# The rows of a small triangular inverse over more slots, and one preparation step a slot later

## The chip, the cores and the metric

The kernel runs on one core of a Trainium2 chip. The metric is the device time of one execution in microseconds (us), as the median over timed runs: 3366.95 us for the kernel before (three runs, 3363.61 to 3374.13). The profiled execution is a run of its own.

## The reference

One layer of a diffusion backbone works on 256 context tokens and 256 latent tokens, each with 2048 channels. It has a feed-forward block (`swiglu_a`), a token mixer, and a second feed-forward block (`swiglu_b`, latent tokens only), each with a modulation in front and a layer norm behind. The change lies in the mixer. There 16 heads of 64 channels run a delta-rule recurrence, over the context tokens first and then over the latent tokens, in both directions (d = 0 forward, d = 1 reverse):

```python
def step(s, inp):
    r_t, v_t, w_t, k_t, a_t, b_t = inp
    sa = jnp.einsum('bhvk,bhk->bhv', s, a_t)
    s = (s * w_t[:, :, None, :] + sa[..., None] * b_t[:, :, None, :]
         + v_t[..., None] * k_t[:, :, None, :])
    return s, jnp.einsum('bhvk,bhk->bhv', s, r_t)
...
for d in range(2):
    s_c, y_c = wkv_scan(r_c, v_c, *dirs_c[d], s_zero, reverse=(d == 1))
    _, y_x = wkv_scan(r_x, v_x, *dirs_x[d], s_c, reverse=(d == 1))
```

Beside the recurrence a gated MLP works on the other 1024 channels, and one projection `w_out` joins both.

## The kernel before, in words

All weights are read as fp32 in 512 KB pieces (`wsplit`): SP loads `raw`, ScalarE (ACT) casts the high part `whi`, VectorE (DVE) makes the low part `wlo`, in the mixer in turn with GpSimd (POOL). Three matmuls (`mm3`, L311 to L313) make one product. There are three buffers of `raw` and four each of `whi` and `wlo`.

In the mixer the recurrence is turned into matrices over chunks of 64 tokens. A *unit* u is one pair of heads t = u // 2 in one direction d = u % 2; there are 16. Each unit passes through three generators:

- `begin(u)` runs `prologue` (d = 0 alone, three slots) and `prep`. `prep` makes decays by a scan (`zp`, `pf`, L732 to L733), exponentials, `kd`, `nb` (L743 to L745), `bk`, `ar`, `wn` (L754 to L770), the products `px` with their masked results `aa` and `ra` (L796 to L806), writes parts of `aa` to DRAM (`scr`, L825) and reads them back, spread over all partitions, as `abc` (L837, 1 MB, one buffer).
- `inverse(u)` inverts the unit-triangular matrices. `small_inverse` does the 16 by 16 blocks row by row on DVE: for each of 15 rows one multiply with `abc` (L851) and one reduce (L852), each needing the row before. Then `Rt` (L865) and four rounds of small matmuls (`pX`, `pR`, L875 to L914) double the size twice and give `R`.
- `finish(u)` runs `solve`: `pu` with `R` (L939), the transition matrices `gi` and `wc` from `pg` (L963 to L976), `pq`, then seven state steps `pS` and `S` (L1004 to L1011) with outputs `y`; for d = 1 also a group norm and the epilogue.

The loop over u runs three of them side by side, `finish(u)`, `begin(u + 2)` and `inverse(u + 1)`, so an even unit holds a d = 0 `finish` and `begin` and a d = 1 `inverse`, an odd unit the opposite. `together` calls each generator once in turn, up to its next `yield`; one such pass is a *slot*, counted from 0. After each slot `burst()` issues some steps of independent matmuls (projections of later heads, the gated MLP, `w_out`) from a queue, so many that the queue should last to the end. At the start of an even unit the projections that its `begin` needs are drained from the queue first. Ahead of the loop a *lead-in* runs `begin(1)` with `inverse(0)`.

The order that each engine sees is set by a planner that starts from the order of the program and its own times; each engine then runs its instructions in that order. `behind()` keeps DVE instructions of `prep` and of the rows after the last instruction marked `urgent` (S, gi, wc, y, aa and a few others). Before the change `inverse` yields twice and then the rows go four to a slot, three in the last:

```python
            if n % 4 == 3:
                yield
```

Of the kernel before, what the change touches and what calls it, by code (L numbers as in the profile page):

```python
# [43 lines left out]
def fl(ap):  # L44
    names = " ".join(f"a{i}" for i in range(len(ap.shape) - 1))
    return ap.rearrange(f"p {names} -> p ({names})")
# [7 lines left out]
def tile_layer(ctx: ExitStack, tc: tile.TileContext, x, c, ctx_in, c_ctx, w_ada, b_ada, ln_g, ln_b,  # L54
# [16 lines left out]
    def ps_v(name):  # L71
        return psum.tile([P, 512], F32, tag="v", name=name, bufs=3)
# [7 lines left out]
    def pre(name, shape=(P, 512), dt=F32):  # L80
        return sp.tile(list(shape), dt, tag="pre", name=name, bufs=PRES)
# [7 lines left out]
    def own(name, shape=(P, 512), dt=F32, bufs=1):  # L89
        return sp.tile(list(shape), dt, tag=name, name=name, bufs=bufs)  # L90
# [610 lines left out]
    def behind():  # L701

        return tc.issue_after(urgent[0].ins) if urgent[0] is not None else nullcontext()
# [11 lines left out]
    def prep(t, d, k, r, kk, vt, ups, kdx, s):  # L715
# [15 lines left out]
        with behind():  # L731
            nc.vector.tensor_reduce(zp[:, :, 0], zp[:, :, 1:L // 2 + 1], axis=AX.X, op=ALU.add, negate=True)  # L732
            nc.vector.tensor_tensor_scan(fl(pf), fl(m65), fl(zp), 0.0, op0=ALU.mult, op1=ALU.add)  # L733
        yield
        sgn = -KAPPA if d == 0 else KAPPA
        e = pre("e", (P, NCH, L + 1))
        nc.scalar.activation(fl(e), fl(pf), AF.Exp, scale=sgn)
# [103 lines left out]
    def small_inverse(d, s):  # L841

        x = own("x16", (P, 8, 16), bufs=2)
        sub = own("a16", (P, 8, 16))
        for z in (x, sub):
            nc.scalar.copy(z, i16.unsqueeze(1).to_broadcast([P, 8, 16]))
        for n, i in enumerate(range(14, -1, -1) if d == 0 else range(1, 16)):
            lo, hi = (i + 1, 16) if d == 0 else (0, i)
            r = slice(i, 16) if d == 0 else slice(0, i + 1)
            with behind():  # L850
                nc.vector.tensor_tensor(sub[:, :, lo:hi], x[:, :, lo:hi], s["abc"][:, i, :, lo:hi], op=ALU.mult)  # L851
                nc.vector.tensor_reduce(x[:, :, i], sub[:, :, r], axis=AX.X, op=ALU.add)  # L852
            if n % 4 == 3:
                yield
        s["x16"] = x

    def inverse(d, s):

        aa = s["aa"]
        for _ in range(2):  # L860
            yield
        yield from small_inverse(d, s)

        Rt = own("Rt", (P, 8, 32))
        nc.vector.tensor_tensor(Rt.rearrange("p j (b t) -> p j b t", t=16), s["x16"].unsqueeze(2).to_broadcast([P, 8, 2, 16]),  # L865
                                mh[:, 0, :].unsqueeze(1).unsqueeze(3).to_broadcast([P, 8, 2, 16]), op=ALU.mult)
        R1 = own("R1", (P, 8, 32))
        nc.vector.transpose(R1, Rt)
        yield
        yield  # L870
        pX = ps_v("pX")
        for i in range(8):
            for b in range(4):
                sb = slice(32 * b, 32 * b + 32)
                nc.tensor.matmul(pX[sb, 32 * i:32 * i + 32], aa[sb, b // 2, i // 4, i % 4, 32 * (b % 2):32 * (b % 2) + 32],  # L875
                                 Rt[sb, i, :], start=True, stop=True)
        Z = own("Z", (P, 8, 32))
        urgent[0] = nc.vector.tensor_tensor(Z, pX[:, 0:256].rearrange("p (i t) -> p i t", t=32),
                                ml[d].unsqueeze(1).to_broadcast([P, 8, 32]), op=ALU.mult)
        yield  # L880
        pR = ps_v("pR")
        for i in range(8):
            for b in range(4):
                sb = slice(32 * b, 32 * b + 32)
                nc.tensor.matmul(pR[sb, 32 * i:32 * i + 32], Z[sb, i, :], R1[sb, i, :], start=True, stop=True)
        nc.vector.tensor_tensor(fl(R1), pR[:, 0:256], fl(R1), op=ALU.add)

        Rt = own("Rt", (P, 8, 32))
        nc.vector.transpose(Rt, R1)
        R = own("R", (P, 8, L))  # L890
        nc.vector.tensor_tensor(R.rearrange("p j (b t) -> p j b t", t=32), R1.unsqueeze(2).to_broadcast([P, 8, 2, 32]),
                                mh[:, 1, :].unsqueeze(1).unsqueeze(3).to_broadcast([P, 8, 2, 32]), op=ALU.mult)
        fa, fb = (0, 32) if d == 0 else (32, 0)
        yield
        pX = ps_v("pX2")
        for i in range(8):
            for q in range(2):
                sa, sb = slice(64 * q + fa, 64 * q + fa + 32), slice(64 * q + fb, 64 * q + fb + 32)
                nc.tensor.matmul(pX[sb, 32 * i:32 * i + 32], aa[sa, q, i // 4, i % 4, fb:fb + 32], Rt[sa, i, :],
                                 start=True, stop=True)  # L900
        Z = own("Z", (P, 8, 32))
        for q in range(2):
            sb = slice(64 * q + fb, 64 * q + fb + 32)
            pz = pX[sb, 0:256].rearrange("p (i t) -> p i t", t=32)
            if q:
                nc.scalar.copy(Z[sb], pz)
            else:
                nc.vector.tensor_copy(Z[sb], pz)
        yield
        pR = ps_v("pR2")  # L910
        for i in range(8):
            for q in range(2):
                sa, sb = slice(64 * q + fa, 64 * q + fa + 32), slice(64 * q + fb, 64 * q + fb + 32)
                nc.tensor.matmul(pR[sa, 32 * i:32 * i + 32], Z[sb, i, :], R1[sb, i, :], start=True, stop=True)  # L914
        for q in range(2):
            sa = slice(64 * q + fa, 64 * q + fa + 32)
            pz = pR[sa, 0:256].rearrange("p (i t) -> p i t", t=32)
            if q:
                nc.scalar.copy(R[sa, :, fb:fb + 32], pz)
            else:  # L920
                nc.vector.tensor_copy(R[sa, :, fb:fb + 32], pz)
        s["R"] = R
# [179 lines left out]
    def begin(u):  # L1102
        t, d = u // 2, u % 2
        if d == 0:
            shared[t] = {}
            yield from prologue(t, shared[t])
        sh = shared[t]
        unit[u] = {}
        yield from prep(t, d, xs[t, 0], xs[t, 2], sh["kk"], sh["vt"], ups[t], sh["kdx"], unit[u])
        yield  # L1110
# [185 lines left out]
    put(gate_low())  # L1296
    gens[1, 2] = put(project(1, 2))
    together(begin(1), inverse(0, unit[0]))
    begun(1)
    gm = []  # L1300
# [3 lines left out]
    for u in range(nu):  # L1304
        t, d = u // 2, u % 2
        pace[0] = left[0] / (nu - u + REST) / SLOTS
        if t + 2 < NRT:
            for i in ((0, 2) if d == 0 else (1,)):
                gens[t + 2, i] = put(project(t + 2, i))
            put(gm.pop(0))  # L1310
        if u == 12:
            drain()
            put(tail())
        chains = [finish(u)]
        if u + 2 < nu:
            if d == 0:
                for i in range(3):
                    drain(gens[t + 1, i])
            chains.append(begin(u + 2))
        if u + 1 < nu:  # L1320
            chains.append(inverse((u + 1) % 2, unit[u + 1]))
        together(*chains)
        if u + 2 < nu:
            begun(u + 2)
# [219 lines left out]
```

## Time and profile before

| | us |
|---|---|
| timed runs, median | 3366.95 |
| profiled execution | 3355.58 |
| its span, first to last instruction | 3353.9 |
| PE busy in the span | 3180.8 |
| mixer's lead-in, from 1745.0 | 50.6 |
| mixer's loop over units, from 1795.6 | 789.4 |

Times in the trace count from the span's start. PE is TensorE, PEld its weight loads, SP the engine that issues nearly all DMAs. "Busy" of PE is the union of its matmuls' spans. The granted clock is the share of full speed that TensorE was given; 1.00 is the 2.4 GHz level and 0.50 the 1.2 GHz level. A line of busy time by stretch has, in this order: the stretch, its length, the busy us of PE, PEld, DVE, ACT and POOL (with the number of instructions), the granted clock, the DMA engines' share, and GB/s. A wait names the instruction that waited and, behind the arrow, the one that ended the wait.

### The profile page before, as it was taken

What the parts mean: (1) busy time and instruction counts of PE and PEld (TensorE: products, weight loads), DVE (VectorE), ACT (ScalarE), POOL (GpSimd) and SP (SyncE); (2) the same over time, 40 slices, a digit from 0 to 9 for tenths busy, and PEclk for the clock granted to TensorE, in tenths of its full rate; (3) what the DMA queues carried; (4) which work ended last, traced back from release to release, by engine and by line L of the source; (5) the groups of instructions that cost most, each with busy time, mean ns of one, the idle gap of its engine ahead of it and who ended that gap; (6) DMA issues with size and microseconds to landing.
All of it is one profiled execution on the core that took longest, in us unless ns stands there. A gap on an engine that the chain in (4) does not pass through costs nothing. (4 is left out here: it accounts for less than half of the span.)

```text
span 3353.9 us, 55585 instructions
## 1 busy us (share of the span) xinstructions
PE 3180.8 (95%) x21224; PEld 2537.6 (76%) x21224; DVE 2111.1 (63%) x4253; ACT 1265.4 (38%) x2225; POOL 437.1 (13%) x393
## 2 busy tenths in 40 slices
PE   8999999999999999999888988898898999999997
PEld 3556877787878878788787777777787888888886
DVE  2345676967557565533867667666776756656568
ACT  2321222222222222222464444544443554444443
POOL 2100000000000000000463333333323000000003
PEclk9999999999999999999988999998898999999999
DMA  8866465757647566433354353434553766666664
GB/s 289 271 201 203 146 177 158 215 168 232 195 145 234 155 192 195 129 94 100 114 158 124 98 120 97 111 97 110 127 128 105 227 209 194 188 189 189 190 188 148
DMA packets 562515, 554.36 MB, mean 165 GB/s; under 512 B 42383, under 2 KB 415284, under 8 KB 560200
## 3 DMA queue, kind: packets, MB, share of 16 engines
q1 hardware_dynamic: 561800, 550.61, 55.0%
q8 instruction: 167, 2.74, 0.3%
q14 instruction: 100, 0.82, 0.1%
q0 software_dynamic: 384, 0.17, 0.0%
q10 hardware_dynamic: 64, 0.02, 0.0%
HBM read 543.35 MB, written 7.35 MB: 164 GB/s over the span
## 5 line engine op out<-in xcount | busy, mean ns | idle before, releaser
L299 ACT CAST whi<-raw 128x512 fp32r<-128x512 f32 (+1 forms) x1366 | 839.4, 618 | 1707.6 <-PE po L312 352.4
L302 DVE TENSOR_TENSOR wlo<-raw,whi 128x512 fp32r<-128x512 f32 (+1 forms) x1188 | 826.2, 698 | 687.8 <-ACT whi L299 678.1
L302 POOL TENSOR_TENSOR wlo<-raw,whi 128x512 fp32r<-128x512 f32 x178 | 240.9, 1356 | 2491.0 <-ACT whi L299 2464.7
L311 PE MATMUL po<-ahi,whi 128*128 128x512 f32 (+1 forms) x768 | 292.6, 381 | 3.8 <-DVE X L417 3.1
L313 PE MATMUL po<-ahi,wlo 128*128 128x512 f32 (+1 forms) x768 | 291.1, 379 | 3.6 <-DVE wlo L302 3.6
L312 PE MATMUL po<-alo,whi 128*128 128x512 f32 (+1 forms) x768 | 292.3, 381 | 0.0
L311 PE MATMUL pgate<-h,whi 128*128 128x512 f32 x704 | 277.9, 395 | 2.0 <-ACT h L307 1.6
L311 PE MATMUL pup<-h,whi 128*128 128x512 f32 x704 | 278.0, 395 | 0.9 <-ACT whi L299 0.9
L313 PE MATMUL pup<-h,wlo 128*128 128x512 f32 x704 | 275.3, 391 | 1.0 <-DVE wlo L302 0.9
L313 PE MATMUL pgate<-h,wlo 128*128 128x512 f32 x704 | 275.1, 391 | 0.2 <-DVE wlo L302 0.2
L312 PE MATMUL pgate<-h,whi 128*128 128x512 f32 x704 | 274.7, 390 | 0.0
L312 PE MATMUL pup<-h,whi 128*128 128x512 f32 x704 | 274.5, 390 | 0.0
L417 DVE SCALAR_TENSOR_TENSOR X<-po,modc,X 128x256 f32<-128x256 f32 x352 | 155.1, 479 | 155.4 <-PE po L313 150.4
L274 DVE SCALAR_TENSOR_TENSOR vt<-xk,wa,vt 128x512 f32<-128x512 f32 x256 | 187.3, 748 | 30.2 <-DMA xk<-in_w_ada_dram 28.5
L311 PEld LDWEIGHTS po<-ahi,whi 128*128 128x128 f32 x768 | 145.9, 190 | 43.3 <-issue 7.7
L274 DVE SCALAR_TENSOR_TENSOR vt<-xv,wa,vt 128x512 f32<-128x512 f32 x224 | 163.7, 748 | 23.2 <-DMA xv<-in_w_ada_dram 21.7
L311 PEld LDWEIGHTS pgate<-h,whi 128*128 128x128 f32 x704 | 132.1, 188 | 53.7 <-ACT whi L299 12.2
L312 PEld LDWEIGHTS po<-alo,whi 128*128 128x128 f32 x768 | 146.0, 190 | 35.2 <-issue 7.5
L311 PEld LDWEIGHTS pup<-h,whi 128*128 128x128 f32 x704 | 132.2, 188 | 51.7 <-ACT whi L299 14.9
L313 PEld LDWEIGHTS po<-ahi,wlo 128*128 128x128 f32 x768 | 146.1, 190 | 33.0 <-DVE wlo L302 4.2
L311 PE MATMUL pp<-h,whi 128*128 128x256 f32 (+1 forms) x448 | 158.6, 354 | 4.1 <-ACT whi L299 2.9
L313 PE MATMUL pp<-h,wlo 128*128 128x256 f32 (+1 forms) x448 | 152.9, 341 | 5.2 <-POOL wlo L302 2.6
(389 smaller groups left out, 6264.0 us busy)
## 6 DMA issues: line engine op xcount, KB each, us to landing
raw<-in_ffn_b_wi_dram SPq DMA_DIRECT2D x176, 512.0 KB
raw<-in_ffn_a_wi_dram SPq DMA_DIRECT2D x156, 512.0 KB
xv<-in_w_ada_dram SPq DMA_DIRECT2D x256, 256.0 KB
xk<-in_w_ada_dram SPq DMA_DIRECT2D x256, 256.0 KB
raw<-in_w_in_dram SPq DMA_DIRECT2D x110, 512.0 KB
raw<-in_ffn_a_wo_dram SPq DMA_DIRECT2D x96, 512.0 KB
raw<-in_ffn_b_wo_dram SPq DMA_DIRECT2D x88, 512.0 KB
abc<-scr SPq DMA_DIRECT2D x16, 1024.0 KB
```

Source lines behind the costliest of these rows:

```text
L274: nc.vector.scalar_tensor_tensor(acc[v], raw, csil[:, kt, v:v + 1], acc[v], op0=ALU.mult, op1=ALU.add)
L299: nc.scalar.copy(hi, r)
L302: (nc.gpsimd if turn[1] and turn[0] % turn[1] == 0 else nc.vector).tensor_tensor(lo, r, hi.bitcast(F32), op=ALU.subtract)
L311: nc.tensor.matmul(o, wh, ah, start=start, stop=False)
L312: nc.tensor.matmul(o, wh, al, start=False, stop=False)
L313: nc.tensor.matmul(o, wl, ah, start=False, stop=stop)
L417: nc.vector.scalar_tensor_tensor(xs, po[:, sl], gc[:, d:d + 1], xs, op0=ALU.mult, op1=ALU.add)
```

## The change

The 15 rows are spread differently, and `prep` yields once more for d = 1, after the scan.

```diff
@@ prep @@
         yield
+        if d == 1:
+            yield
         sgn = -KAPPA if d == 0 else KAPPA
...
@@ small_inverse @@
-            if n % 4 == 3:
+            if n + 1 in ((3, 6, 9, 12) if d == 0 else (3, 5, 8, 11, 13)):
                 yield
...
@@ inverse @@
-        for _ in range(2):
-            yield
+        if d == 0:
+            for _ in range(3):
+                yield
         yield from small_inverse(d, s)
```

By slot:

| | before | after, d = 0 | after, d = 1 |
|---|---|---|---|
| rows in slot 0, 1, 2, ... | 0, 0, 4, 4, 4, 3 | 0, 0, 0, 3, 3, 3, 3, 3 | 3, 2, 3, 3, 2, 2 |
| `Rt` in slot | 5 | 7 | 5 |
| `pX`, `pR`, `pX2`, `pR2` in slots | 7 to 10 | 9 to 12 | 7 to 10 |
| `prep`, d = 1: scan; `kd`; `bk`, `ar`; `aa` in slots | 0; 1; 2; 4 and 5 | | 0; 2; 3; 5 and 6 |
| `prep`, d = 1: `scr`; `abc` in slots | 6; 7 | | 7; 8 |
| `prep`, d = 0: scan; `kd`; `bk`, `ar`; `aa` in slots | 3; 4; 5; 7 and 8 | as before | |

## Rows read from the trace of the kernel before

**Rows 1.** The page: busy time of the engines; granted clock in 40 slices.
```profile
PE 3180.8 (95%) x21224; PEld 2537.6 (76%) x21224; DVE 2111.1 (63%) x4253; ACT 1265.4 (38%) x2225; POOL 437.1 (13%) x393
PEclk9999999999999999999988999998898999999999
```

**Rows 2.** Busy time by stretch (columns above): lead-in, mixer's loop.
```profile
1745.00:1795.60 50.60, 41.00 (x515) 34.40 (x511) 36.20 (x85) 20.54 (x38) 16.00 (x14) 0.90 0.51 116
1795.60:2585.00 789.40, 701.58 (x9643) 589.44 (x9642) 543.93 (x1576) 366.08 (x694) 259.91 (x227) 0.94 0.44 112
```

**Rows 3.** PE's waits in the mixer's loop: us in total, times, longest.
```profile
PE pS L1004 <- DVE S L1011: 13.3, 11, 2.3
...
PE px L796 <- DVE ar L764: 9.1, 4, 3.1
...
PE pX L875 <- DVE Rt L865: 6.5, 7, 2.2
...
PE px L796 <- DVE a L851: 4.3, 2, 3.2
...
PE px L796 <- DVE x L852: 2.1, 3, 1.4
...
PE pS L1004 <- DVE x L852: 1.3, 1, 1.3
PE pu L939 <- issue: 0.8, 1, 0.8
```

**Rows 4.** PE's waits in the lead-in.
```profile
PE px L796 <- DVE aa L806: 7.4, 2, 5.8
```

**Rows 5.** DVE in order of time in unit 2: start, us, instruction.
```profile
1926.38 1.16 DVE L851 TENSOR_TENSOR a<-x,abc 128x80 f32<-128x80 f32 x1
...
1927.73 0.48 DVE L743 TENSOR_SCALAR kd<-ic,hcol 128x512 f32<-128x512 f32 x1
...
1930.66 0.73 DVE L851 TENSOR_TENSOR a<-x,abc 128x96 f32<-128x96 f32 x1
1931.31 0.90 DVE L764 TENSOR_TENSOR ar<-xr,e 128x256 f32<-128x256 f32 x1
```

**Rows 6.** PE in order of time, same place; in brackets the idle time before.
```profile
1932.36 0.68 PE L796 MATMUL px<-ar,bk 64*128 64x128 f32 x6 [2.79 <-DVE ar L764]
```

**Rows 7.** Busy time and granted clock around that wait (columns as above).
```profile
1926.00:1933.00 7.00, 4.21 (x39) 3.13 (x37) 6.93 (x19) 3.63 (x7) 3.72 (x4) 1.00 0.25 77
1933.00:1939.80 6.80, 6.80 (x109) 5.33 (x108) 4.02 (x15) 0.59 (x2) 1.99 (x2) 0.50 0.06 19
```

**Rows 8.** DVE's groups, 1795.6 to 2530: busy us, mean ns, idle before.
```profile
L851 DVE TENSOR_TENSOR a<-x,abc 128x8 f32<-128x8 f32 (+14 forms) x225 | 83.2, 370 | 2.3
...
L852 DVE TENSOR_REDUCE x<-a 128x8 f32<-128x16 f32 (+14 forms) x225 | 49.7, 221 | 2.6
```

**Rows 9.** DVE in order of time: the last reduce of unit 3's inverse.
```profile
1987.01 0.28 DVE L852 TENSOR_REDUCE x<-a 128x8 f32<-128x128 f32 x1
```

**Rows 10.** SP in order of time, units 1 and 3: issues of DMAs.
```profile
1886.00 0.63 SPq L837 DMA_DIRECT2D abc<-scr  x1
...
1981.08 5.09 SPq L825 DMA_DIRECT2D scr<-aa  x8
...
1987.66 0.80 SPq L837 DMA_DIRECT2D abc<-scr  x1
1988.51 9.26 SPq L294 DMA_DIRECT2D raw<-in_w_in_dram  x2
```

**Rows 11.** Busy time by stretch behind that load of unit 1 (columns as above).
```profile
1889.00:1898.00 9.00, 6.52 (x111) 4.50 (x101) 3.58 (x16) 0.98 (x2) 0.70 (x1) 0.81 0.53 126
1898.00:1900.00 2.00, 1.26 (x7) 0.73 (x5) 1.63 (x2) 0.36 (x1) 1.57 (x2) 1.00 0.00 0
```

**Rows 12.** DVE in order of time at the start of unit 4 (from 2000.3).
```profile
2006.45 0.69 DVE L302 TENSOR_TENSOR wlo<-raw,whi 128x512 fp32r<-128x512 f32 x1 [5.02 <-ACT whi L299]
2009.89 1.00 DVE L659 SCALAR_TENSOR_TENSOR xk<-pp,mus,xk 128x255 f32<-128x255 f32 x2 [2.75 <-ACT xk L656]
```

## The prediction

> **What bounds the kernel now.** I read the page first, then the table by stage, then who waits for whom on PE, then the order of instructions around single waits. On the page PE is busy 95% of the span and the digit of its granted clock falls to 8 in five slices alone, all of them between 21 and 31 (1677 to 2599 us) [rows 1]. The stage table says why: in the mixer's main loop, 789.4 us long, PE is busy 701.6 us, so 87.8 us are idle, and the mean clock is 0.94, which takes another (1 - 0.94) x 789.4 = 47 us of full speed. DVE is busy 544 us there, 69%, POOL 260, and the stage of the lead-in (50.6 us) has 9.6 us of idle PE at a clock of 0.90 [rows 2]. Nothing is saturated on average: the loop is bound by PE waiting for single results that stand late in DVE's order. The list of PE's waits in the loop is short and has the small inverse all through it [rows 3]: px waits for `ar` (9.1 us, four times) and for the rows themselves (4.3 and 2.1), the state step pS waits for S (13.3, eleven times) and once for a row (1.3), and pX waits for Rt (6.5), which follows the last row. These are 36.6 us of the 87.8. In the lead-in px waits 7.4 us for aa, behind which rows stand as well [rows 4].
>
> One wait shown: DVE runs a row's multiply and reduce from 1926.38, then kd and nb, then another multiply at 1930.66, and only then `ar` at 1931.31 [rows 5]; PE starts px at 1932.36 after 2.79 us idle [rows 6]. The stretch up to there has a granted clock of 1.00 (the 2.4 GHz level), the next 6.8 us has 0.50 (the 1.2 GHz level), with PE busy all through it [rows 7]. So that stall cost 2.8 us of idle time and 3.4 us of clock. Over the loop the relation is smaller: 47 us of clock for 87.8 us idle, 0.54 us per us. I use that.
>
> **The change, part by part.** It removes no instruction and adds none: 225 multiplies at 370 ns and 225 reduces at 221 ns [rows 8] stay on DVE, so a row costs 0.59 us and the 15 rows of one inverse 8.9 us. What moves is the slot (a pass of `together`). A unit has 13 slots (d = 1), 12 (d = 0) or 11 (the last d = 0), 199 in all, so a slot is 789.4 / 199 = 4.0 us. These counts don't change: finish(d = 1) with its 13 sets the odd units before and after, begin(d = 0) with its 12 the even ones. The lead-in gets 13 slots in place of 11; the ten more matmul triples that it issues are taken from unit 0's drain, so I cost that at nothing.
>
> *Rows of the d = 1 inverse (even units).* Before: 4, 4, 4 and 3 rows in slots 2 to 5, on top of the scan (slot 3), kd and nb (4), bk, ar and wn (5). After: 3, 2, 3, 3, 2, 2 in slots 0 to 5. By the time `ar` is traced, 13 rows are behind it in the program and they began two slots sooner; before it was 12 rows, late. In the wait shown rows take 1.35 us (1926.38 to 1927.73) and 0.65 us (1930.66 to 1931.31) of what stands before `ar`: 2.0 of 2.79 us, 72%. I take 72% of the 9.1 us: 6.5.
> *Fewer rows a slot, both directions.* Four rows are 2.4 us of a 4.0 us slot; three are 1.8, two and a half 1.5. That is 25 to 38% less ahead of S, of the px that wait for rows, and of Rt. I take 30% of 13.3 + 1.3 + 4.3 + 2.1 + 6.5 = 27.5: 8.3. Below, nothing (the waits stay and name another instruction); above, half (13.8).
> *Lead-in.* The same 30% of 7.4: 2.2; bounds 0 and 3.7.
> *Preparation of d = 1 one slot later.* kd and nb leave slot 1, where gi and wc stand. PE's wait for wc isn't among the longer ones, so nothing there; bk, ar and aa meet three rows a slot in place of four, which is counted above.
> Idle time saved: 6.5 + 8.3 + 2.2 = 17.0 us; with 0.54 for the clock 26.2 us.
>
> *What is late next: the load of abc.* abc has one buffer, so the load for the d = 1 inverse waits on SP for the last row of the d = 0 inverse in the same odd unit, and SP's weight loads queue behind it. Now the last reduce is at 1987.01 [rows 9] and the load is issued at 1987.66, right behind the scr writes, with the next weights after it [rows 10]: those two already meet. After, the d = 0 rows end in slot 7, not 5, and the load is traced in slot 8, not 7. So the load goes later by 4 us (one slot) to 8 us (two slots); I take 6, because three rows a slot should lag less than four. A load is slow: the one issued at 1886.00 filled 1889 to 1898 at 126 GB/s, and then the DMA engines are empty [rows 10, 11], so it takes about 12 us from issue to landing. From 1987.66 that lands at about 2000, where the even unit begins; 6 us later it lands at 2006. Its first three rows (1.8 us) now are traced in slot 0. DVE is idle there for 5.0 us up to a wlo at 2006.45, and then until 2009.89 [rows 12], so the first rows would have been free had abc been there. With abc at 2006 they run until 2007.8 and hold that wlo by about 1.3 us less the 0.3 that it can start early: 1.0 us. Seven odd units issue such a load (the eighth is the lead-in's): 7 x 1.0 x 1.54 = 10.8 us. Below, 0 (four us later: the rows fit into the idle stretch). Above, eight us later with all five rows of slots 0 and 1 in front of the wlo: 1.6 + 2.5 = 4.1 us, x 1.54 x 7 = 44 us.
> The page "DMA: Bandwidth & Descriptors" of the Trainium skill, section "Anatomy of one DMA", would have the load cheaper: about 2.0 us fixed and the bytes at 436 GB/s (fitted for DMAs issued by POOL, this one is SP's), an estimate of 4.4 us for 1 MB. By it abc would land well ahead of the even unit, this cost would be 0, and the sum 10.8 us better. The trace here has 9 us of transfer alone [rows 11], and I go by it.
>
> *The d = 0 chain ends in slot 12, not 10.* R's last copies now come right before the next unit's pu. PE waited for the start of pu once, 0.8 us [rows 3]; the drained matmuls stand beside it. I take one more such wait, 0.8 x 1.54 = 1.2; bounds 0 and seven of them, 8.6.
>
> **Sum.** -26.2 + 10.8 + 1.2 = -14.2 us on the profiled execution, 3355.6 us, of which the span is 3353.9: 3341.4. The median of the three timed runs is 3366.95, 11.4 us above the profiled one, so the timed median becomes 3353.
>
> **Rivals.**
> *The waits only move.* DVE's order is the planner's: rows of slot 4 (80 and 96 wide) already stand interleaved with kd, nb and bk [rows 5]. Rows that leave one slot are then set in front of something else, and the list changes its names and not its sum. For it: pS waits eleven times, 1.2 us each, on a chain of its own, and most of the DVE work in the loop isn't rows (133 of 544 us). Against it: 2.0 us of rows stood in front of `ar` in plain sight. It leaves between the lead-in's 2 us and a third of the gain, set off by the late load: -5 to +5, 3362 to 3372.
> *abc decides (slower).* One mechanism: the load lands after DVE's first wlo of the even unit is due, DVE stands still at the head of its order with a row that waits for data, and PE's drained matmuls run out of wlo. It decides from a landing about 6 us after the unit's start. At two slots' delay it costs up to 44 us against 26 gained: +18, 3385; with the gain at half, +31, 3398. For it: the two events already touch [rows 9, 10], and the transfer is slow. Against it: POOL makes every second wlo, four are buffered, and the planner may put the rows behind the wlo.
> *More than counted.* Each of the longer stalls is followed by a halved clock; with the upper bounds of the savings and no late load it is (9.1 + 13.8 + 3.7) x 1.54 = 41 us, 3326.
>
> **How the numbers follow.** Forecast, with its own range of 3334 to 3360: 0.56, of which 0.08 lies less than 0.3% (10 us) below before, which is about what a measurement of this kernel can tell from no change. Waits only move: 0.22, all but 0.02 of it within 0.3%. abc decides: 0.18, of which 0.02 within and the rest slower. More than counted: 0.04, faster. Faster is 0.48 + 0.02 + 0.04 = 0.54, within 0.08 + 0.20 + 0.02 = 0.30, slower 0.16. The range for 8 in 10 leaves out the top of the late-load case and the bottom of the last one: 3333 to 3376.
>
> **What would show it.** Right: px's waits for `ar` fall under 4 us in the list, pS's under 11, the loop's idle PE under 76 us and its clock reaches 0.95 or more; the first rows of even units stand before gi in DVE's order. The cost shows as DVE waiting for a DMA of abc at L851 (no such wait is in the trace now) and as wlo waits of pp early in even units. Wrong: idle PE in the loop as before with other names; or pu and pX waiting together more than the 17 us saved.

## The result and the profile after

The changed kernel is slower: 3389.6 us, the median of five runs (3381.4 to 3396.8), beside 3366.95 us for five runs of the kernel before; the ratio is 1.0067, with a 95% interval of 1.0048 to 1.0086. The forecast was 3353, with a range of 3333 to 3376: the direction and the range both missed. The profiled execution's span is 3380.7 us, before 3353.9. In the changed kernel the lines stand two or three further down: the rows' multiply is L853 and reduce L854 (before L851, L852), `px` L798, `pu` L942, R's last copy L924, the load of `abc` L839.

The page, as in [rows 1]:

```profile
PE 3192.2 (94%) x21224; PEld 2545.7 (75%) x21224; DVE 2096.2 (62%) x4253; ACT 1264.0 (37%) x2223; POOL 438.7 (13%) x393
PEclk9999999999999999999898989988999999999999
```

Busy time by stretch, lead-in and loop, as in [rows 2] (the same columns):

```profile
1745.00:1800.60 55.60, 41.73 (x504) 35.06 (x504) 35.08 (x87) 20.97 (x38) 14.64 (x13) 0.89 0.53 121
1800.60:2615.30 814.70, 712.74 (x9642) 597.01 (x9642) 533.16 (x1582) 366.54 (x693) 261.31 (x228) 0.92 0.42 108
```

The lead-in is 5.0 us longer and the loop 25.3. In the loop PE's idle time went from 87.8 to 102.0 us (814.70 - 712.74), which is 14.1 us, and its busy time for the same matmuls from 701.6 to 712.7, which is 11.2 us of lower clock (0.92 for 0.94). What follows the loop is 3.5 us shorter (2615.3 to 3380.7; before 2585.0 to 3353.9). Together +26.8 us, the whole difference of the spans.

PE's waits in the loop, as in [rows 3]:

```profile
PE pu L942 <- DVE R L924: 28.7, 7, 5.9
PE px L798 <- POOL ar L759: 8.4, 6, 3.8
...
PE pS L1007 <- DVE S L1014: 5.8, 11, 1.3
...
PE pX L878 <- DVE Rt L868: 4.6, 7, 1.0
PE pX L902 <- DVE Rt L892: 4.5, 4, 1.6
...
PE px L798 <- DVE ar L766: 3.3, 2, 2.0
...
PE px L798 <- DVE x L854: 3.1, 3, 2.3
```

DVE's waits over lead-in and loop:

```profile
DVE a L853 <- DMA abc<-scr: 47.6, 8, 7.4
```

The first line of the first list is new: `pu`, the first matmuls of a unit's `finish`, waits seven times for R's last copy. (The first of the seven ends the lead-in, so its 5.9 us lie in the lead-in's length.) The line of DVE is new too: in all eight d = 1 inverses DVE stands still for `abc`. Seven of the eight go with the seven waits of `pu`; in unit 12 `pu` doesn't wait. This is DVE in order of time at the start of unit 2 (start, us, instruction; in brackets the idle time before it and what ended it):

```profile
1901.84 0.48 DVE L1096 SCALAR_TENSOR_TENSOR y<-pgb,pcol,bon 128x256 f32<-128x256 f32 x1
1907.43 0.17 DVE L853 TENSOR_TENSOR a<-x,abc 128x8 f32<-128x8 f32 x1 [5.11 <-DMA abc<-scr]
1907.54 0.48 DVE L1100 SCALAR_TENSOR_TENSOR o<-y,pcol,pgt 128x256 f32<-128x256 f32 x1
1907.94 0.42 DVE L1072 TENSOR_TENSOR bon<-pb,xv 128x256 f32<-128x256 f32 x1
1908.27 0.40 DVE L924 COPY R<-pR 32x256 f32<-32x256 f32 x1
```

PE in order of time there:

```profile
1902.54 0.69 PE L917 MATMUL pR<-R,Z 32*32 32x32 f32 x32
...
1908.73 4.07 PE L942 MATMUL pu<-rhs,R 64*64 64x128 f32 x32 [4.60 <-DVE R L924]
```

The issue of the load, on SP:

```profile
1894.67 0.62 SPq L839 DMA_DIRECT2D abc<-scr  x1
```

`pR` is done at 1903.23, and R's copy needs nothing else. But in DVE's list the first row of the next inverse stands ahead of it, with `o` and `bon` between, and DVE runs its list in order. The row waits for the load issued at 1894.67 and starts at 1907.43; R follows 0.84 us later, and PE, whose own list goes on with `pu`, starts it after 4.60 us idle. The stretch behind it runs at half the clock (last columns: granted clock, DMA share, GB/s):

```profile
1901.00:1907.90 6.90, 3.12 (x63) 2.15 (x57) 1.37 (x4) 0.98 (x2) 0.00 (x0) 1.00 0.77 131
1907.90:1914.70 6.80, 5.97 (x37) 5.26 (x38) 2.08 (x9) 2.36 (x7) 0.00 (x0) 0.50 0.14 43
```

The load and R's chain start from the same event, the last row of the d = 0 inverse (1894.4). R's chain takes 8.8 us from there (to 1903.2), the load 12.8 us from its issue to the row (12.8 to 13.8 over the eight d = 1 inverses). Whatever is ready when `pR` is done and lies behind the row in DVE's list comes some 4 us late or more; R's copy starts 5.0 us after `pR`'s end.

### The profile page after: what moved, and what is told of

Same layout as the page of the kernel before. It is cut to its first block, busy times and chain, and to the rows that moved or that the text cites. A ratio compares the mean times of both kernels' runs of the same rounds, so it can differ in the third digit from the quotient of the medians.

```text
span 3380.7 us, 55595 instructions
## 1 busy us (share of the span) xinstructions
PE 3192.2 (94%) x21224; PEld 2545.7 (75%) x21224; DVE 2096.2 (62%) x4253; ACT 1264.0 (37%) x2223; POOL 438.7 (13%) x393
```

## The experiments

All ratios are to the kernel before, timed beside each, with 95% intervals; shares in us are taken of 3357. The kernel before takes 3356 to 3359 us in these runs, not 3366.95, so a time that was expected in us is to be read as a ratio to 3366.95. "Changed" is the kernel just described.

**R's copy ahead of the row.** In the changed kernel R's copy is marked `urgent`, so the rows of the next inverse are placed behind it.

```diff
-                nc.vector.tensor_copy(R[sa, :, fb:fb + 32], pz)
+                urgent[0] = nc.vector.tensor_copy(R[sa, :, fb:fb + 32], pz)
```

> The changed kernel, with R's last copy on DVE marked urgent, so that the rows of the next inverse stay behind it; no slot moves. Theory A (the loss is DVE's order: the first row of the d = 1 inverse waits for abc in front of R's copy, and pu waits for R): pu's waits for R (28.7 us, 7 times) fall under 5, the time falls by 28.7 x 1.54 = 44 us from 3389.6 to about 3346, DVE's wait for abc stays at some 25 to 48 us but costs little. Rival B (R is late because the d = 0 chain ends in slot 12): pu still waits over 20 us, time 3380 to 3395. Rival C (the block itself costs, by the wlo behind it): pu's waits go, waits for wlo early in the even units take their place with 10 to 20 us, time 3365 to 3385.

Measured 0.9954 [0.9936, 0.9972]: faster than before by 15 us. The waits of `pu` for R are gone, though the d = 0 chain ends where it did, against rival B. DVE still waits for `abc`, and waits for `wlo` (6.6 us in the loop, 7.9 in the changed kernel) don't take the place of `pu`'s, against rival C. DVE's wait over lead-in and loop:

```profile
DVE a L853 <- DMA abc<-scr: 33.4, 8, 6.3
```

DVE in order of time at the start of unit 2:

```profile
1898.21 0.41 DVE L924 COPY R<-pR 32x256 f32<-32x256 f32 x1
1903.07 0.17 DVE L853 TENSOR_TENSOR a<-x,abc 128x8 f32<-128x8 f32 x1 [4.44 <-DMA abc<-scr]
```

The loop, as in [rows 2]:

```profile
1798.40:2572.30 773.90, 697.81 (x9644) 584.78 (x9644) 539.67 (x1584) 366.35 (x692) 259.74 (x228) 0.94 0.44 114
```

DVE stands still for 4.44 us all the same, with R already copied. Its idle time by itself costs little; what costs is R behind it. The profiled span is 43.7 us shorter than the changed kernel's (3337.0 for 3380.7), for 28.7 us of waits taken away: 1.52 us per us, about the 1.54 that the forecast used. These are two single traces; the timed ratios differ by 0.0113, with an interval of some 0.0026 either way, that is 38 us (29 to 47) where 44 were expected, or 1.3 us per us.

**The load in halves.** In the changed kernel `abc` is loaded by two DMAs of 512 KB, the half with the first rows ahead; nothing is marked.

```diff
-        nc.sync.dma_start(abc.rearrange("p s j t -> p (s j t)"),
-                          scr.rearrange("(g s) c -> g (s c)", g=8).unsqueeze(1).to_broadcast([8, 16, 2048]))
+        for hv in ((0, 1) if d == 1 else (1, 0)):
+            nc.sync.dma_start(abc[:, 8 * hv:8 * hv + 8].rearrange("p s j t -> p (s j t)"),
+                              scr.rearrange("(g s) c -> g (s c)", g=8)[:, 1024 * hv:1024 * hv + 1024].unsqueeze(1).to_broadcast([8, 16, 1024]))
```

> The changed kernel with the load of abc issued as two DMAs of 512 KB, the half with the inverse's first rows ahead. Theory A (DVE stands at the first row until the 1 MB load has landed, and R's copy stands behind it): the first half lands some 5 us after its issue in place of 9 to 11, DVE's waits for abc fall from 47.6 us to 10 to 20, pu's waits for R from 28.7 to under 10, and the ratio to the kernel before is 0.993 to 1.000. Theory B (not the load: R's own chain ends later by two slots, and its copy would be late without the row ahead of it): pu's waits for R stay over 20 us and the ratio at 1.004 to 1.008.

Measured 0.9951 [0.9935, 0.9967]. DVE's waits for `abc` fall to 7.6 us, `pu`'s for R to 0.5. At the start of unit 2 the row still stands ahead of R's copy, and the wait is nearly gone, because the load was issued at 1887.78 and the row runs 6.8 us later (in the changed kernel 12.8), just as `pR` is done (1894.72). DVE there, and PE's `pR`:

```profile
1894.59 0.17 DVE L854 TENSOR_TENSOR a<-x,abc 128x8 f32<-128x8 f32 x1 [0.78 <-DMA abc<-scr]
1894.69 0.48 DVE L1101 SCALAR_TENSOR_TENSOR o<-y,pcol,pgt 128x256 f32<-128x256 f32 x1
1895.09 0.42 DVE L1073 TENSOR_TENSOR bon<-pb,xv 128x256 f32<-128x256 f32 x1
1895.42 0.40 DVE L925 COPY R<-pR 32x256 f32<-32x256 f32 x1
```

```profile
1894.03 0.69 PE L918 MATMUL pR<-R,Z 32*32 32x32 f32 x32
```

So the cause needs both halves, a row ahead of R's copy and a load that lands later than R's chain. Either removed gives the same time, within the intervals.

**Both at once.** Load in halves and R's copy urgent.

> The load in two halves, as in the run before it, and R's copy urgent, so that no row is planned ahead of it. Theory A says that either alone takes away most of one and the same wait, so both together bring little more than R's copy alone, which gave 0.9954: 0.991 to 0.996, DVE's waits for abc under 20 us, pu's for R under 3. If the two add up (0.988 or less), the late load had a second cost of its own beside pu's wait.

Measured 0.9942 [0.9920, 0.9964]: the two don't add up. The late load had no second cost that these runs can tell.

**One slot's distance.** In the changed kernel the d = 1 inverse starts in slot 1, not 0.

```diff
-        if d == 0:
-            for _ in range(3):
+        for _ in range(3 if d == 0 else 1):
```

> The changed kernel with the d = 1 inverse starting in slot 1 in place of slot 0 (rows 3, 2, 3, 3, 2, 2 in slots 1 to 6). Theory A: the first row stands behind gi and wc, abc has landed by then, DVE waits for abc under 3 us in all, pu's waits for R under 5 us; 3340 to 3355. Rival B: pu waits for R over 20 us as the d = 0 chain is untouched; 3380 to 3395. Rival C says as A here.

Measured 0.9982 [0.9965, 1.0000]. DVE's waits for `abc` are 2.0 us, and `pu` doesn't wait for R: one slot is room enough for the load. The waits are as theory A said, the time isn't: 3340 to 3355 meant 0.992 to 0.9965. It is less good than the runs above, though the cost is as gone here; why stays open.

**Without the d = 1 part.** In the changed kernel the d = 1 inverse goes back to slots 2 to 5 with 4, 4, 4 and 3 rows; the d = 0 spread and the later preparation stay.

```diff
-            if n + 1 in ((3, 6, 9, 12) if d == 0 else (3, 5, 8, 11, 13)):
+            if n + 1 in ((3, 6, 9, 12) if d == 0 else (4, 8, 12)):
...
-        if d == 0:
-            for _ in range(3):
+        for _ in range(3 if d == 0 else 2):
```

> The d = 0 half of the change and the later preparation alone: the d = 1 inverse as before (rows 4, 4, 4, 3 from slot 2). Theory A: no wait for abc at the head of DVE's order, pu's waits gone; the gain of the fewer rows in odd units and the lead-in alone remains, 3352 to 3365. Rival B: pu waits for R over 20 us; 3385 to 3400.

Measured 0.9931 [0.9906, 0.9956], 3337.4 us: the fastest of all, 23 us under the kernel before, though the runs with the wait taken away (0.9942 to 0.9954) lie within its interval. `pu` doesn't wait for R. The expected 3352 to 3365, 0.9956 to 0.9994, was too cautious.

**The other parts, alone and in pairs.** "Spread d = 0" is its three slots of delay with three rows a slot; "slot 0" is the d = 1 inverse from slot 0 with 3, 2, 3, 3, 2, 2 rows, so its start and its grouping together; "later prep" is the added `yield`. The edits are the change's own lines, put in or left out.

> The d = 1 half of the change and the later preparation alone: the d = 0 inverse as before (rows 4, 4, 4, 3 from slot 2, R's last copy in slot 10). Theory A: R's copy stands ahead of the first row, pu's waits for R gone; DVE may still wait for abc in front of the last steps of the group norm, up to 3 us a unit; 3350 to 3368. Rival B says pu's waits go as well, 3345 to 3360. Rival C (blocked DVE costs by itself): 3365 to 3385.

> Both inverses as changed, the preparation of d = 1 as before. Theory A (cost: the first row in slot 0 stands at the head of DVE's order before its abc has landed, with R's copy or the last steps of the group norm behind it): DVE waits for abc 35 to 60 us in all, as the load still waits for the d = 0 rows; pu waits 20 to 35 us; ratio to before 1.000 to 1.012. Rival D (the later preparation is what makes the load late): DVE waits for abc under 15 us, ratio 0.990 to 0.998.

> The kernel before with the d = 1 inverse alone as changed (rows 3, 2, 3, 3, 2, 2 from slot 0). Neither the d = 0 rows nor the preparation are later, so the load is issued when it was. Theory A: the load still lands after the first row's place in DVE's order; DVE waits for abc 20 to 45 us, pu 10 to 25 us, ratio 0.998 to 1.006. Rival D and the prediction's own step (the load must first become later): DVE waits for abc under 8 us, ratio 0.992 to 0.998.

> The kernel before with the d = 0 inverse alone as changed (three rows a slot in slots 3 to 7). Theory A: no wait for abc at DVE's head (under 3 us); the gain of run e3_d1_old (0.9931) was the d = 0 spread's: ratio 0.992 to 0.996. Rival E (that gain was the later preparation's): ratio 0.998 to 1.001.

> The kernel before with the later preparation of d = 1 alone. Theory A: ratio 0.998 to 1.001, px's waits for ar move but stay within 3 us of before. Rival E (the gain of e3_d1_old was this): ratio 0.992 to 0.996.

| parts | ratio | 95% |
|---|---|---|
| spread d = 0 | 0.9979 | 0.9963 to 0.9994 |
| later prep | 0.9977 | 0.9962 to 0.9993 |
| spread d = 0, later prep | 0.9931 | 0.9906 to 0.9956 |
| slot 0 | 1.0050 | 1.0031 to 1.0069 |
| slot 0, later prep | 1.0024 | 1.0007 to 1.0041 |
| slot 0, spread d = 0 | 1.0102 | 1.0081 to 1.0124 |
| all three (the change) | 1.0067 | 1.0048 to 1.0086 |

Slot 0 costs in all four pairs of rows: 0.0050 alone, 0.0047 beside the later preparation, 0.0123 beside the d = 0 spread, 0.0136 beside both, that is 16 to 46 us. Of the 0.0136, 0.0113 goes with R's copy out of the row's way (0.9954), and what is left, 0.0023, isn't clear of the intervals; for the other pairs no run takes the start apart from the grouping. The other two parts gain 0.002 each and 0.007 together; that they gain more together than summed isn't clear of the intervals either.

So 0.9931 is neither the d = 0 spread's alone nor the later preparation's: both came out between the two ranges expected for them. Slot 0 alone, and slot 0 with the d = 0 spread, came out as theory A said: DVE waits 29.2 and 50.5 us for `abc`, `pu` 17.0 us in all and 29.5 us for R. The first speaks against the prediction's own step that the load must first become later. Slot 0 with the later preparation lies above theory A's time as a ratio (up to 1.0003) and within rival C's: DVE waits 50.3 us for `abc`, up to 9.6 at once.

The victim isn't always R's copy. With slot 0 and the later preparation, where the d = 0 rows end in slot 5 as before, R's copy stands ahead of the row; behind it stands `y`, which reads `pgb` out of the PSUM buffers that `pu` takes in turn, and `pu` waits for `y`. DVE of that kernel at the start of unit 2:

```profile
1906.68 0.17 DVE L853 TENSOR_TENSOR a<-x,abc 128x8 f32<-128x8 f32 x1 [8.05 <-DMA abc<-scr]
1907.10 0.17 DVE L853 TENSOR_TENSOR a<-x,abc 128x16 f32<-128x16 f32 x1
1907.19 0.48 DVE L1095 SCALAR_TENSOR_TENSOR y<-pgb,pcol,bon 128x256 f32<-128x256 f32 x1
```

PE there:

```profile
1907.72 1.97 PE L941 MATMUL pu<-rhs,R 64*64 64x128 f32 x16 [7.08 <-DVE y L1095]
```

There `pu` waits 25.0 us for `y`, in five times:

```profile
PE pu L941 <- DVE y L1095: 25.0, 5, 8.4
```

With slot 0 alone it waits for either:

```profile
PE pu L939 <- DVE y L1093: 12.4, 4, 3.7
...
PE pu L939 <- DVE R L921: 4.6, 1, 4.6
```

In that kernel the load isn't traced later than before; a row in slot 0 needs no later load to come too early. A wait at the head of DVE's list is paid for by whoever needs what stands behind it.

**Fewer rows a slot, without slot 0.** The fastest version, with the d = 1 rows three a slot from slot 2.

```diff
-            if n + 1 in ((3, 6, 9, 12) if d == 0 else (4, 8, 12)):
+            if n + 1 in (3, 6, 9, 12):
```

> The d = 0 inverse and the preparation of d = 1 as in the changed kernel; the d = 1 inverse starts in slot 2 as before, but with rows 4, 4, 4, 3 by row number (a slot ends behind row 4, 8 and 12), against three a slot, in the version that gave 0.9931 with the old grouping. Theory A: no row is planned ahead of the landed load, so DVE's waits for abc stay under 3 us and pu never waits for R. If fewer rows a slot alone made the gain, a different grouping moves the ratio by 0.002 or more; if not, it stays within 0.002 of 0.9931.

The text on record names the two groupings the wrong way round: this kernel has three rows a slot, the version of 0.9931 has 4, 4, 4 and 3. Measured 1.0001 [0.9984, 1.0017]. DVE doesn't wait for `abc`, nor `pu` for R, as expected; but the grouping moved the time by 0.007, against the d = 1 spread. The loop of the version of 0.9931, as in [rows 2]:

```profile
1793.40:2566.50 773.10, 697.65 (x9650) 581.12 (x9649) 536.35 (x1588) 366.65 (x694) 264.18 (x230) 0.95 0.45 115
```

The loop of this one:

```profile
1792.60:2582.70 790.10, 713.99 (x9642) 592.47 (x9641) 539.66 (x1579) 365.97 (x692) 263.57 (x227) 0.92 0.43 112
```

PE idles 75.5 us in the one and 76.1 in the other; of the 17.0 us between them 16.3 are busy time, at a granted clock of 0.95 and 0.92. Why the second is granted less for as much idle time stays open: these are single traces, though the timed ratios stand apart too.

## Why the prediction was wrong

**The failed step is the price of the late load, 10.8 us ("hold that wlo by ... 1.0 us").** It set the landing against the first `wlo` of the even unit, because DVE was idle up to there [rows 12], and never asked what else DVE had to hand to PE at the unit's start: R's copy, and the `y` that frees PSUM. The waits taken away by the first experiment measure it at 28.7 us idle in seven units, 4.1 us each where 1.0 was forecast, and with its clock at 43.7 us by the traces and 38 by the timed ratios. The upper bound of that term had the same 4.1 us and 44 us, worked out for a load eight us late with five rows ahead of a `wlo`. That the size was in the text, by another cause, is luck, and too little of the range was given to it.

**The two costs were summed, though they are one.** "R's last copies now come right before the next unit's pu" was priced at 1.2 us with a bound of 8.6, the load apart from it. Both edits, the d = 0 rows two slots later and the d = 1 row in slot 0, bring R's copy and the waiting row together; the table of parts shows it: 0.0050 alone, 0.0123 to 0.0136 with the d = 0 spread.

**The load goes later: right, and not what decided.** Counted from the start of `pu` of its odd unit, the issue is 1.2 to 10.9 us later than before, 5.4 on the mean of the seven, for 6 forecast. With slot 0 alone it is 1.0 later on the mean, and that costs 0.0050 all the same. The load's 12 us stood in [rows 10, 11]; how long R's chain is behind the same last row was never read.

**The load is slow: right.** 12.8 us from issue to row in unit 2, beside the 12 taken from the trace. By the Trainium skill, page "DMA: Bandwidth & Descriptors", section "Anatomy of one DMA", about 4.4 us was the estimate; it would have set the landing, and with it the row, ahead of `pR`'s end. This case's measurement decides, 12.8 us.

**Savings, 17.0 us of idle time and 26.2 us in all: some six tenths.** The first experiment has the whole change without the wait of `pu`. Its span is 16.9 us under before's, its time 15 us by the ratio; idle time in lead-in and loop is 86.1 us for 97.4, 11.3 saved of 17.0.
- *`ar`, 6.5 forecast: failed.* The wait for DVE's `ar` fell from 9.1 to 3.3 us, under the 4 that was to show it right; but PE now waits 8.4 us for POOL's half of `ar`, which no long wait of before names: 11.7 us for both halves. The longest of these, in unit 6 (PE in order of time):

```profile
2154.66 1.22 PE L798 MATMUL px<-ar,bk 64*128 64x128 f32 x6 [3.85 <-POOL ar L759]
```

  The same place in the kernel before, which waited for DVE's half: PE, and POOL's half:

```profile
2129.24 0.68 PE L796 MATMUL px<-ar,bk 64*128 64x128 f32 x6 [3.08 <-DVE ar L764]
```

```profile
2127.95 0.86 POOL L757 TENSOR_TENSOR ar<-kk,e 128x256 f32<-128x256 f32 x1
```

  POOL's half had ended at 2128.81, 0.43 us ahead of PE's start. So of 3.08 us an earlier DVE half could bring 0.4 there, and the 72% left out the second engine. That is "the waits only move", at this place.
- *Fewer rows a slot, 8.3 forecast: more.* `pS`'s wait for S went from 13.3 to 5.8 us, `px` for rows from 6.4 to 3.1, `pX` for Rt from 6.5 to 4.6 with a new 4.5 behind the second transpose. All in all 27.5 us became 18.2 (5.8, 0.2 for a row, 3.1, 4.6, 4.5), 9.3 less, in one trace of each. The spread of d = 0 does most for S: alone it takes it to 7.2 us; the later preparation alone to 11.1. For d = 1 three rows a slot showed no gain (last experiment).
- *Lead-in, 2.2 forecast:* `px`'s waits there are 6.2 us after 7.4 [rows 4], 1.2 less; R's first wait of 5.9 us then made it longer.

**0.54 us of clock per us idle:** it fits this cost (0.52 by the traces; 0.3, with 0.0 to 0.6 as interval, by the timed ratios), but not as a rule: of two kernels with 75.5 and 76.1 us idle one runs 16.3 us longer busy.

**The rival that held** was the load deciding, chance 0.18: DVE at the head of its order with a row that waits for data, PE waiting behind it, 3385 with the gain in full. Half of its mechanism came true: DVE stands still and PE waits behind it, but for R, where the text had the drained matmuls out of `wlo`; no wait of `pp` for `wlo` is in the loop's list. Its time came nearly (3389.6), partly by luck: it set 44 us against 26 gained, where the traces have 43.7 against 16.9. Its condition, a landing 6 us after the unit's start, didn't arise: the row runs 1.3 us ahead of unit 2's `pu`, which waits for R. And against it stood "the planner may put the rows behind the wlo"; it didn't.

## What to carry to other kernels

Work that waits for a DMA and is moved into an engine's idle stretch costs nothing only if nothing that another engine needs comes behind it in that engine's list before the data have landed: list all of that, not the next instruction of the idle stretch alone. When a load and a chain start from the same event, compare their lengths first (here 12.8 and 8.8 us), and either keep the chain's last step ahead of the load's first reader or split the load. Where several edits go in together, run each part alone: here two parts in three gained 0.7%, and the third turned that into a loss of 0.7%.

## What the runs showed beside

Two kernels with the same matmuls and the same idle time in the loop (75.5 and 76.1 us, one trace of each) were granted 0.95 and 0.92 of the clock, worth 16.3 us of PE's busy time: idle time alone doesn't tell what the clock will cost. And the first half of the 1 MB load, issued as two DMAs back to back, could be used 6.6 to 8.0 us after the issue (the five times that DVE waited for it), the whole, as one DMA, after 12.8 to 13.8.
